# Two transformer blocks on one core: the first attention with stationary values and its softmax factors spread through DRAM, and single operations moved

## The chip, the cores and the metric

The kernel runs on one core of a Trainium2 chip. The metric is the device time of one execution in microseconds; the core's engines (TensorE for matrix products, VectorE, ScalarE, GpSimd, and SyncE, here SP, which issues nearly all DMAs) run beside each other, each in its own program order, and wait for each other by semaphores. A time is the median of several executions; one further execution is recorded by the hardware profiler, and the rows in this document come from it.

## The reference, cut to what matters

All data are float32: 1024 tokens of width 1024.

```python
# first block
h = rms_norm(x, norm_mix);  proj = h @ w_in          # aq ak av rq rk rv rg ga gr
att = sliding_window_attention(aq, ak, av, sinks)    # 8 heads of 64, 2 kv heads, window 128, alibi,
                                                     # softmax with a sink logit in the denominator
ret = head_group_norm(retention_chunkwise(rq, rk, rv)) * gain * silu(rg)
x = x + (sigmoid(ga) * (att @ w_att_o) + sigmoid(gr) * (ret @ w_ret_o)) @ w_out
h = rms_norm(x, norm_ffn)
x = rms_norm(x + (silu(h @ w_gate) * (h @ w_up)) @ w_down, final_norm)
# second block
z = rms_norm(x, g_pre_mix) @ w_in_2                  # q k v zu zv
attn = dilated_attention(q, k, v, rel_bias)          # T5 bias by relative position
sgu = spatial_gating(gelu(zu), gelu(zv), ...)
x = x + rms_norm(concat(attn, sgu) @ w_out_2, g_post_mix)
f = square(relu(rms_norm(x, g_pre_ffn) @ w_ff1)) @ w_ff2
out = x + rms_norm(f, g_post_ffn)
```

## The kernel before

**Products.** Each large product is done in three passes of a split format: an operand is cast to a high part (ScalarE, `split`, L279) and the rest is subtracted (VectorE, L281, names `wl`, `midl`), and TensorE multiplies high with high, high with low and low with high. On top of this the products use a seven-product (Strassen-like) scheme: of the 2 by 2 blocks of weights and activations, sums and differences are formed first. In `s_run` (L504 and on, matmuls at L500 to L502) the weights stand still in TensorE and the pieces are numbered 1 to 7; in `d_run` (L1169 and on, matmuls at L1199 to L1201) four accumulators run through pieces in an order given by a tuple, ORD_S, ORD_M or ORD_V. One piece of `d_run` is 48 matmuls of 512 columns.

**Weights.** `plan` lists all weight chunks (1 MB each) and pieces in the order of their use. There are two raw buffers; a chunk is loaded as soon as a buffer is free (`load_raw`, L299). A piece is split when the product before it has left room (`ahead`), at a `tick`; operations marked late are appended to a list that `flush` empties. `d_chunks` writes the combinations for one such product: `t1`, the first difference `wt = raw(0,1) - raw(0,0)`; at piece 6 `wt = raw(1,1) - wt`; at piece 3 a difference in place; and for the two orders in which piece 2 comes before piece 6 ("apart") a fourth block `wr`, loaded separately, and `t4`, `wr = wr - wt`. All of these are VectorE's, L440 in the trace. Activations of the down-projections go through DRAM: `mid_d` is stored by SP, `midr` loaded (`a_load`, L1107), and `a_split` forms their combinations (`mt`, L1138 to L1144).

**Order of work.** Nothing is scheduled by a tool: each engine's order is the order in which the code emits. Smaller work is a set of generators, and `pump` moves each of them one step, newest first, at fixed places between the large products. SP's queue is in order too: a DMA that waits for its data holds back those behind it.

**First attention.** `att1_quad` (L1275 and on) treats one block of 128 queries and four heads: 16 quads, 8 blocks by two head groups. Each goes through four steps, one per pump: scores and softmax (reductions on VectorE, L1290, exponentials on ScalarE, L1293); reciprocal of the sums (`den`, L1300) and transposes of the probabilities (L1306) into `pT`; the product with the values, `pv` (L1319), with the transposed probabilities stationary and 64 columns of values moving, and the scaling by `den` out of PSUM (L1322); two transposes of the result (L1328), a cast and a subtraction to the split format. The quads run beside the projections of retention's queries and keys (`t_unit`), with two pumps per half. The attention's output product (`ao`) comes after the retention has been begun.

**The other places that the change touches.** `bias_build` (L1420) makes the table of relative biases, stores it and copies it in DRAM to 128 rows per head (L1436) during the first FFN's `s_run`. The second FFN's `s_run` is followed by the last down-projection, four chunks e0, e8, e16 and e24. `out_chain` (L1794) is the last normalization: `osq`, `rv` and `rw` on GpSimd (L1783, L614, L615), the result on VectorE, ScalarE and GpSimd.

Of the kernel before, what the change touches and what calls it, by code (L numbers as in the profile page):

```python
# [175 lines left out]
class Kern:  # L176
# [150 lines left out]

    def get(self, key):
        while key not in self.ready:
            self.flush()  # L330
            self.split_next()
        if key in self.open:
            self.flush()
        self.n_used += 1
        return self.ready.pop(key)
# [89 lines left out]
    def d_chunks(self, w, k0, m, key, order, cols=(0, 512), n=512, late=False):  # L425
# [11 lines left out]
        if late:  # L437
            at[5] = (0, 0)
# [12 lines left out]
        def piece(p, j):  # L451
# [10 lines left out]
            def emit(r):  # L462
# [4 lines left out]
                if apart and p == (5 if late else order[1]):  # L467
# [3 lines left out]
                elif p == 3:  # L471
                    sub(blk(0, 1), blk(1, 1), blk(0, 1))
                src = (tmp[j] if p in (5, 6) or p == 4 and not apart else own[j] if p == 4 or p == 2 and apart
# [4 lines left out]
                if apart and p == 6:  # L478
# [3 lines left out]
                elif not apart and p == 1:  # L482
# [152 lines left out]
    def plan(self):  # L635
# [25 lines left out]
        self.d_chunks(a["w_ret_o"][0], 0, 4, "ro", ORD_S)  # L661
        self.d_chunks(a["w_out"][0], 0, 4, "wo", ORD_S)
# [10 lines left out]
        self.d_chunks(w2, 0, 4, "vz", ORD_V, (1024, 2048))  # L673
# [4 lines left out]
        self.d_chunks(a["w_ff1_2"][0], 0, 4, "ff", ORD_V)  # L678
# [3 lines left out]
        for k0, m in self.echunks:  # L682
            self.d_chunks(a["w_ff2_2"][0], k0, m, f"e{k0}", ORD_M)
# [296 lines left out]
    def ffn1(self, X, x1_d):  # L980
# [59 lines left out]
        for i in range(4, DFF // P, 2):  # L1040
# [5 lines left out]
            n - 7: self.bias_build,  # L1046
# [228 lines left out]
    def att1_quad(self, n, u, aq, ak, av, att):  # L1275
# [24 lines left out]
        nc.vector.reciprocal(den, den)  # L1300
        pT = self.S("pT", [P, 8, P])
# [10 lines left out]
        yield  # L1312
        pv = self.PV("pv")
        for s in range(2):
            for j in range(2):
                x = 2 * s + j
                for e in range(nh):
                    kb = n - nh + 1 + e
                    nc.tensor.matmul(pv[:, 64 * x : 64 * x + 64], pT[:, x * nh + e, :],  # L1319
                                     av[:, kb * P + 64 * s : kb * P + 64 * s + 64], start=(e == 0), stop=(e == nh - 1))  # L1320
        at = self.H("at", [P, 2, 2, 64])
        nc.vector.tensor_tensor(  # L1322
            at.rearrange("p j s d -> p s j d"), pv[:, 0:256].rearrange("p (s j d) -> p s j d", s=2, j=2),
            den.rearrange("p (s j) -> p s j", s=2)[:, :, :, None].to_broadcast([P, 2, 2, 64]), ALU.mult)
        yield
        tp = self.PM("tq").rearrange("p (a b) -> p a b", b=P)
        for j in range(2):
            nc.tensor.transpose(tp[:, j, :], at[:, j].rearrange("p s d -> p (s d)"), self.ident)  # L1328
        hi, lo = att.pair(u, n // 4)
        att.missing.discard(2 * n + u)  # L1330
        o = (n % 4) * P
        nc.scalar.copy(hi[:, :, o : o + P], tp[:, 0:2, :])
        nc.vector.tensor_tensor(lo[:, :, o : o + P], tp[:, 0:2, :], hi[:, :, o : o + P].bitcast(F32), ALU.subtract)
# [86 lines left out]
    def bias_build(self):  # L1420
        nc, a, dp = self.nc, self.a, self.dp
# [5 lines left out]
        nc.sync.dma_start(rw, a["c_row"].partition_broadcast(8))  # L1427
        R = self.S("R", [8, L_BIAS])
# [4 lines left out]
        d1 = dp.tile([8, L_BIAS], F32, name="bias_d1")  # L1433
        nc.sync.dma_start(d1, R)
        d2 = dp.tile([8, P, L_BIAS], F32, name="bias_d2")
        nc.sync.dma_start(d2, bass.AP(tensor=d1.tensor, offset=d1.offset, ap=[[L_BIAS, 8], [0, P], [1, L_BIAS]]))  # L1436
        self.bias_d = d2
# [287 lines left out]
    def ffn2(self, X, x3_d, turned):  # L1725
# [28 lines left out]
        self.d_queue(mid_d, [(k0, k0, m, ORD_M, False) for k0, m in self.echunks])  # L1754
# [243 lines left out]
```

## Time and profile before

| | us |
|---|---|
| median of three executions | 2555.37 |
| lowest and highest | 2554.02, 2561.91 |
| profiled execution, its own time | 2560.22 |
| its span | 2558.4 |

The span runs from the first to the last instruction that the profiler shows. Times in rows count from its start. "Busy" of TensorE (PE) is the time in which a matmul is under way; matmuls are pipelined, so the distance between two starts tells their cost better than one's duration. A row of the timeline gives start, duration, engine, source line, operation, result and operands, shape and count, and in brackets how long the engine had been idle before and whom it waited for. PEclk is the granted clock of TensorE as a share of 2.4 GHz.

### The profile page before, as it was taken

How to read it: one execution, taken by the hardware profiler on the slowest of the kernel's cores; microseconds unless marked ns; L12 is line 12 of the kernel's file. 1: busy time of each engine (PE TensorE's matmuls, PEld its weight loads, DVE VectorE, ACT ScalarE, POOL GpSimd, SP SyncE). 2: the span in 40 equal slices, each digit the busy share in tenths (PEclk: the TensorE clock that was granted, in tenths of full speed). 3: DMA queues.
4: the chain of work that ended last, by engine and by line, in shares of the span. 5: the costliest groups of instructions: out<-in, count | busy, mean ns of one | idle time of the engine just before them, and what ended most of it. 6: DMA issues, size and time to landing. Idle time of an engine off the chain costs nothing.

```text
span 2558.4 us, 31387 instructions
## 1 busy us (share of the span) xinstructions
PE 2488.2 (97%) x11889; PEld 2060.4 (81%) x11889; DVE 1753.5 (69%) x2741; ACT 1141.1 (45%) x1960; POOL 186.9 (7%) x252
## 2 busy tenths in 40 slices
PE   7999999999999999999999999999999999899998
PEld 5888888888778888878788877889887888788886
DVE  7654456556899845555799986666458444488888
ACT  5444445412425433333334544576436555553334
POOL 1000000000002000000000311023320000000006
PEclk9999999999999999999999999999999999999999
DMA  4233333135353122242433414233242333532334
GB/s 157 95 115 107 118 109 108 34 106 186 112 197 132 58 74 83 74 151 95 169 126 137 137 50 160 86 81 100 88 148 90 108 104 105 179 115 75 115 124 148
DMA packets 194239, 291.58 MB, mean 114 GB/s; under 512 B 27752, under 2 KB 102136, under 8 KB 194088
## 3 DMA queue, kind: packets, MB, share of 16 engines
q1 hardware_dynamic: 191784, 287.41, 33.2%
q10 hardware_dynamic: 2304, 2.16, 0.3%
q8 instruction: 94, 1.54, 0.2%
q14 instruction: 57, 0.47, 0.1%
HBM read 212.89 MB, written 80.31 MB: 115 GB/s over the span
## 4 chain that ended last, share of the span: by engine, by line
PE 75%; DVE 14%; DMA 5%; ACT 3%; issue 2%; POOL 1%; SPq 0%; DVEq 0%; ACTq 0%; POOLq 0%
PE a L500 6%; PE a L501 6%; PE a L502 6%; PE da L1201 5%; PE da L1200 5%; PE da L1199 5%; DVE wl L281 3%; PE b L501 3%; PE b L500 3%; PE b L502 3%; PE db L1200 3%; PE db L1201 3%; PE db L1199 3%; PE pv L1944 2%; DVE midl L281 2%
## 5 line engine op out<-in xcount | busy, mean ns | idle before, releaser
L500 PE MATMUL a<-midh,ws 128*128 128x512 f32 x708 | 276.6, 391 | 9.8 <-DVE f L1733 8.8
L502 PE MATMUL a<-midh,ws 128*128 128x512 f32 x708 | 276.2, 390 | 0.0
L501 PE MATMUL a<-midl,ws 128*128 128x512 f32 x708 | 276.1, 390 | 0.0
L1201 PE MATMUL da<-wh,midl 128*128 128x512 f32 x624 | 245.6, 394 | 6.3 <-DVE midl L281 6.2
L1200 PE MATMUL da<-wl,midh 128*128 128x512 f32 x624 | 245.0, 393 | 3.6 <-DVE wl L281 3.6
L1199 PE MATMUL da<-wh,midh 128*128 128x512 f32 x624 | 246.5, 395 | 0.8 <-ACT midh L279 0.8
L279 ACT CAST midh<-mt 128x1024 fp32r<-128x1024 f32 x80 | 82.9, 1036 | 246.1 <-DVE mt L1138 97.6
L1201 PE MATMUL db<-wh,midl 128*128 128x512 f32 x436 | 170.4, 391 | 2.9 <-DVE midl L281 2.8
L1199 PE MATMUL db<-wh,midh 128*128 128x512 f32 x436 | 170.4, 391 | 1.4 <-ACT midh L279 1.3
L1200 PE MATMUL db<-wl,midh 128*128 128x512 f32 x436 | 170.1, 390 | 1.6 <-DVE wl L281 1.6
L500 PEld LDWEIGHTS a<-midh,ws 128*128 128x128 f32 x708 | 133.4, 188 | 39.3 <-issue 9.6
L502 PEld LDWEIGHTS a<-midh,ws 128*128 128x128 f32 x708 | 133.3, 188 | 27.8
L501 PEld LDWEIGHTS a<-midl,ws 128*128 128x128 f32 x708 | 133.4, 188 | 27.6
L279 ACT CAST ws<-tc 128x512 fp32r<-128x512 f32 x180 | 111.4, 619 | 88.4 <-DVE tc L414 87.2
L1201 PEld LDWEIGHTS da<-wh,midl 128*128 128x128 f32 x624 | 117.9, 189 | 34.7 <-DVE midl L281 10.4
L1200 PEld LDWEIGHTS da<-wl,midh 128*128 128x128 f32 x624 | 118.1, 189 | 29.1 <-DVE wl L281 5.2
L500 PE MATMUL b<-midh,ws 128*128 128x512 f32 x360 | 140.0, 389 | 0.0
L501 PE MATMUL b<-midl,ws 128*128 128x512 f32 x360 | 140.0, 389 | 0.0
L502 PE MATMUL b<-midh,ws 128*128 128x512 f32 x360 | 140.0, 389 | 0.0
L1199 PEld LDWEIGHTS da<-wh,midh 128*128 128x128 f32 x624 | 118.1, 189 | 26.9 <-ACT midh L279 1.7
L281 DVE TENSOR_TENSOR wl<-raw,wh 128x1024 fp32r<-128x1024 f32 x117 | 136.3, 1199 | 3.7 <-ACT wh L279 3.6
L279 ACT CAST wh<-raw 128x1024 fp32r<-128x1024 f32 x121 | 120.7, 1037 | 39.5 <-DMA raw<-in_w_ff_dram 20.7
(352 smaller groups left out, 5772.5 us busy)
## 6 DMA issues: line engine op xcount, KB each, us to landing
raw<-in_w_ff_dram SPq DMA_DIRECT2D x31, 1024.0 KB, 5.1
mid_d<-f SPq DMA_DIRECT2D x108, 256.0 KB, 2.3
midr<-mid_d SPq DMA_DIRECT2D x52, 512.0 KB, 7.2
raw<-in_w_in_dram SPq DMA_DIRECT2D x22, 1024.0 KB, 5.4
x<-x_d SPq DMA_DIRECT2D x24, 512.0 KB, 5.2
raw<-in_w_up_dram SPq DMA_DIRECT2D x11, 1024.0 KB, 5.6
raw<-in_w_gate_dram SPq DMA_DIRECT2D x10, 1024.0 KB, 5.3
xt<-in_x_dram SPq DMA_DIRECT2D x16, 512.0 KB, 10.9
```

Source lines behind the costliest of these rows:

```text
L279: self.nc.scalar.copy(hi, s)
L281: e.tensor_tensor(lo, s, hi.bitcast(F32), ALU.subtract)
L500: nc.tensor.matmul(ps, hi[:, i], xh, start=(first and i == 0), stop=False, skip_group_check=True)
L501: nc.tensor.matmul(ps, hi[:, i], xl, start=False, stop=False, skip_group_check=True)
L502: nc.tensor.matmul(ps, lo[:, i], xh, start=False, stop=(i == 3), skip_group_check=True)
L1199: nc.tensor.matmul(ps, xh, wh, start=(kt == 0 and p in (1, 5, 2)), stop=False, skip_group_check=True)
L1200: nc.tensor.matmul(ps, xh, wl, start=False, stop=False, skip_group_check=True)
L1201: nc.tensor.matmul(ps, xl, wh, start=False, stop=(kt == m - 1), skip_group_check=True)
L1944: nc.tensor.matmul(pv[:, 65 * x : 65 * x + 65], pT[0:w, 2 * x + e, :], vv[0:w, 65 * x : 65 * x + 65], start=(e == 0), stop=(e == 1))
```

## The change

In the first attention the values become the stationary operand: for each of the two key blocks (`e`) and each half (`s`) one matmul loads 64 columns of values into one half of TensorE's columns, writes 64 partitions of the result, and has 256 columns of transposed probabilities moving. The result comes out feature by token, so the transposes at the end go away. The factor `den` belongs to the token, which is now the free dimension; it is stored to DRAM, transposed by the store, and loaded back spread over 64 partitions per half. ScalarE copies the product out of PSUM, and in the next step VectorE multiplies it with the factors.

Outside the attention: `t4` is put off to piece 7 for `ro`, `wo` and `ff` (`defer`); `t1` is put off to piece 5 for `vz` and `ff` (`late`) and for the first chunk of the last down-projection, e0 (`lazy`); pieces of e0 from number 5 on are not split before the `s_run` ahead of it has ended (`hold`, `release`), and the six activation loads in its last pair become two, with four in `release`; the bias table is fetched, built and spread in separate steps, the spread head by head; in the last normalization the scaling of the first half's sum is folded into a scaling of the gain.

```diff
@@ Kern
+    def hold(self, key):
+        self.cap = next(i for i, p in enumerate(self.pieces) if p[0] == key)
+
+    def release(self, n):
+        self.cap = 10 ** 9
+        self.flush()
+        self.load_raw(10 ** 9)
+        self.a_load(n)
@@ d_chunks
-    def d_chunks(self, w, k0, m, key, order, cols=(0, 512), n=512, late=False):
+    def d_chunks(self, w, k0, m, key, order, cols=(0, 512), n=512, late=False, lazy=False, defer=False):
...
-        if late:
+        if late or lazy:
             at[5] = (0, 0)
...
-                if apart and p == (5 if late else order[1]):
+                if apart and p == (5 if late else order[1]) or lazy and p == 5:
                     t1()
...
+                elif p == 7 and defer:
+                    sub(own[j], own[j], tmp.pop(j))
...
-                if apart and p == 6:
+                if apart and p == 6 and not defer:
                     def t4(t=tmp.pop(j)):
                         sub(own[j], own[j], t)
                     self.late.append(t4)
-                elif not apart and p == 1:
+                elif not apart and p == 1 and not lazy:
                     t1()
@@ plan
-        self.d_chunks(a["w_ret_o"][0], 0, 4, "ro", ORD_S)
-        self.d_chunks(a["w_out"][0], 0, 4, "wo", ORD_S)
+        self.d_chunks(a["w_ret_o"][0], 0, 4, "ro", ORD_S, defer=True)
+        self.d_chunks(a["w_out"][0], 0, 4, "wo", ORD_S, defer=True)
-        self.d_chunks(w2, 0, 4, "vz", ORD_V, (1024, 2048))
+        self.d_chunks(w2, 0, 4, "vz", ORD_V, (1024, 2048), late=True)
-        self.d_chunks(a["w_ff1_2"][0], 0, 4, "ff", ORD_V)
+        self.d_chunks(a["w_ff1_2"][0], 0, 4, "ff", ORD_V, late=True, defer=True)
-            self.d_chunks(a["w_ff2_2"][0], k0, m, f"e{k0}", ORD_M)
+            self.d_chunks(a["w_ff2_2"][0], k0, m, f"e{k0}", ORD_M, lazy=k0 == 0)
@@ ffn1
-            n - 7: self.bias_build,
+            n - 14: self.bias_fetch,
+            n - 13: self.bias_build,
+            **{n - 12 + h: (lambda h=h: self.bias_spread(h)) for h in range(8)},
@@ att1_quad
         nc.vector.reciprocal(den, den)
+        fac_d = self.dp.tile([4, P], F32, name=f"fac_d{u}_{n}")
+        nc.sync.dma_start(fac_d.rearrange("x q -> q x"), den)
...
         pv = self.PV("pv")
-        for s in range(2):
-            for j in range(2):
-                x = 2 * s + j
-                for e in range(nh):
-                    kb = n - nh + 1 + e
-                    nc.tensor.matmul(pv[:, 64 * x : 64 * x + 64], pT[:, x * nh + e, :],
-                                     av[:, kb * P + 64 * s : kb * P + 64 * s + 64], start=(e == 0), stop=(e == nh - 1))
-        at = self.H("at", [P, 2, 2, 64])
-        nc.vector.tensor_tensor(
-            at.rearrange("p j s d -> p s j d"), pv[:, 0:256].rearrange("p (s j d) -> p s j d", s=2, j=2),
-            den.rearrange("p (s j) -> p s j", s=2)[:, :, :, None].to_broadcast([P, 2, 2, 64]), ALU.mult)
+        for e in range(nh):
+            kb = n - nh + 1 + e
+            for s in range(2):
+                nc.tensor.matmul(pv[64 * s : 64 * s + 64, 0:256], av[:, kb * P + 64 * s : kb * P + 64 * s + 64],
+                                 pT[:, 2 * nh * s + e : 2 * nh * (s + 1) : nh, :], start=(e == 0), stop=(e == nh - 1))
+        both = self.H("at", [P, 2, 2, P])
+        at, fac = both[:, 0], both[:, 1]
+        nc.scalar.copy(at, pv[:, 0:256].rearrange("p (j q) -> p j q", j=2))
+        nc.sync.dma_start(fac, bass.AP(tensor=fac_d.tensor, offset=fac_d.offset, ap=[[2 * P, 2], [0, 64], [1, 2 * P]]))
         yield
-        tp = self.PM("tq").rearrange("p (a b) -> p a b", b=P)
-        for j in range(2):
-            nc.tensor.transpose(tp[:, j, :], at[:, j].rearrange("p s d -> p (s d)"), self.ident)
-        hi, lo = att.pair(u, n // 4)
+        nc.vector.tensor_tensor(at, at, fac, ALU.mult)
+        hi, lo = (x[:, :, (n % 4) * P : (n % 4) * P + P] for x in att.pair(u, n // 4))
         att.missing.discard(2 * n + u)
-        o = (n % 4) * P
-        nc.scalar.copy(hi[:, :, o : o + P], tp[:, 0:2, :])
-        nc.vector.tensor_tensor(lo[:, :, o : o + P], tp[:, 0:2, :], hi[:, :, o : o + P].bitcast(F32), ALU.subtract)
+        nc.scalar.copy(hi, at)
+        nc.vector.tensor_tensor(lo, at, hi.bitcast(F32), ALU.subtract)
@@ bias_build, split into bias_fetch (three loads), bias_build and
+    def bias_spread(self, h):
+        d1 = self.bias_row
+        self.nc.sync.dma_start(self.bias_d[h], bass.AP(tensor=d1.tensor, offset=d1.offset + h * L_BIAS, ap=[[0, P], [1, L_BIAS]]))
@@ ffn2
+        self.hold("e0:5_0")
         self.s_run(X.ops, pairs, {
...
-            len(pairs) - 1: lambda: self.a_load(6)})
+            len(pairs) - 1: lambda: self.a_load(2)})
         self.ahead, self.a_ahead = 2, 4
         X.keep.clear()
+        self.release(4)
...
                 gpo = self.bcast("gpo2", a["g_post_ffn_2"][0])
+                nc.scalar.activation(gpo, gpo, AF.Copy, scale=32.0)
...
-                    nc.gpsimd.tensor_scalar(q[:, 0:1], q[:, 0:1], 1.0 / D, EPS, op0=ALU.mult, op1=ALU.add)
@@ out_chain
-        r = yield from self.rstd(sq[:, 1:2], 1, 1.0 / D, sq[:, 0:1])
+        v, r = self.M("rv", 1), self.M("rw", 1)
+        nc.gpsimd.tensor_scalar(v, sq[:, 1:2], sq[:, 0:1], D * EPS, op0=ALU.add, op1=ALU.add)
+        nc.gpsimd.tensor_tensor(r, v, self.mhalf[:, :1], ALU.pow)
+        yield
```

## Rows read from the trace of the kernel before

**Rows 1.** The page, part 1: busy time, share of the span and instructions of TensorE

```profile
PE 2488.2 (97%) x11889; PEld 2060.4 (81%) x11889; DVE 1753.5 (69%) x2741; ACT 1141.1 (45%) x1960; POOL 186.9 (7%) x252
```

**Rows 2.** Windows, attention stage: length; busy PE, PEld, DVE, ACT, POOL; clock, DMA share, GB/s

```profile
418.00:500.00 82.00, 82.00 (x566) 72.52 (x566) 46.36 (x181) 40.84 (x147) 0.00 (x0) 1.00 0.08 27
```

**Rows 3.** Timeline of PE, the end of one quad's pump in the attention

```profile
444.18 1.90 PE L1319 MATMUL pv<-av,pT 128*128 128x64 f32 x16
445.91 0.39 PE L1328 MATMUL tq<-ident,at 128*128 128x128 f32 x2
446.06 0.48 PE L581 MATMUL mm<-zh,wh 128*128 128x512 f32 x1
```

**Rows 4.** Timeline of PE: column halves in the second block; full width in the retention

```profile
525.17 0.60 PE L1374 MATMUL po<-rvh,sd 128*128 128x256 f32 x2
525.61 0.59 PE L1376 MATMUL po<-st,qd 128*128 128x256 f32 x2
...
1547.71 1.09 PE L1845 MATMUL sgu<-wsT,yp 128*64 128x128 f32 x16
1548.73 0.50 PE L1199 MATMUL da<-wh,midh 128*128 128x512 f32 x1
```

**Rows 5.** Timeline of DVE: the reciprocals of two quads that follow each other

```profile
438.72 0.18 DVE L1300 RECIPROCAL den<-den 128x4 f32<-128x4 f32 x1
...
445.36 0.18 DVE L1300 RECIPROCAL den<-den 128x4 f32<-128x4 f32 x1
```

**Rows 6.** DMA issues: line, queue, count, KB each, median us from issue to landing

```profile
mid_d<-f SPq DMA_DIRECT2D x108, 256.0 KB, 2.3
midr<-mid_d SPq DMA_DIRECT2D x52, 512.0 KB, 7.2
```

**Rows 7.** Timeline of PE: hand-over to the last down-projection, first and second product

```profile
2234.67 0.76 PE L500 MATMUL a<-midh,ws 128*128 128x512 f32 x1 [8.82 <-DVE f L1733]
...
2238.22 0.63 PE L502 MATMUL a<-midh,ws 128*128 128x512 f32 x1
...
2239.42 0.40 PE L1199 MATMUL da<-wh,midh 128*128 128x512 f32 x1
...
2250.33 0.39 PE L1199 MATMUL db<-wh,midh 128*128 128x512 f32 x1
```

**Rows 8.** Timeline of DVE at the hand-over

```profile
2232.70 1.23 DVE L440 TENSOR_TENSOR wt<-raw,raw 128x1024 f32<-128x1024 f32 x1 [9.46 <-DMA raw<-in_w_ff_dram]
```

**Rows 9.** Timeline of SP at the hand-over

```profile
2216.70 3.83 SPq L1107 DMA_DIRECT2D midr<-mid_d  x6
...
2221.43 0.39 SPq L299 DMA_DIRECT2D raw<-in_w_ff_dram  x1
```

**Rows 10.** Windows at the hand-over, columns as in rows 2

```profile
2234.00:2238.00 4.00, 3.33 (x8) 2.68 (x9) 2.84 (x3) 3.41 (x5) 0.00 (x0) 0.50 0.17 66
```

**Rows 11.** Timeline of DVE, first projection of the second block

```profile
1468.98 2.36 DVE L440 TENSOR_TENSOR wt<-raw,raw 128x1024 f32<-128x1024 f32 x2
```

**Rows 12.** Timeline of PE, first projection of the second block

```profile
1471.73 0.44 PE L140 MATMUL tp<-ident,xn 128*128 128x128 f32 x2 [1.82 <-DVE zr L146]
```

**Rows 13.** Timeline of DVE, before the second FFN

```profile
1923.48 1.29 DVE L1716 SCALAR_TENSOR_TENSOR x<-y,rw,x 128x1024 f32<-128x1024 f32 x1 [0.44 <-POOL rw L615]
```

**Rows 14.** Timeline of DVE, retention's output projection

```profile
682.75 1.22 DVE L440 TENSOR_TENSOR wr<-wr,wt 128x1024 f32<-128x1024 f32 x1
```

**Rows 15.** Timeline of PE, retention's output projection

```profile
685.16 0.50 PE L1200 MATMUL da<-midl,wh 128*128 128x512 f32 x1 [3.12 <-DVE midl L281]
```

**Rows 16.** Waits of DVE, 685 to 800: us in total, times, longest us

```profile
DVE midl L281 <- ACT midh L279: 4.7, 6, 1.2
```

**Rows 17.** Timeline of PE in the first FFN

```profile
1140.97 0.50 PE L500 MATMUL c<-zh,ws 128*128 128x512 f32 x1 [1.09 <-ACT ws L279]
```

**Rows 18.** Timeline of DVE at the end

```profile
2547.01 0.76 DVE L1803 SCALAR_TENSOR_TENSOR yg<-yg,rw,x 128x512 f32<-128x512 f32 x1 [2.33 <-POOL rw L615]
```

**Rows 19.** Timeline of POOL at the end

```profile
2542.25 0.51 POOL L1783 TENSOR_SCALAR osq<-osq 128x1 f32<-128x1 f32 x1
```

More of the change, by code (lines that the diff above doesn't have):

```diff
@@ L1417, in retention, with bias_fetch @@
         return [vload()] + [chunk(c) for c in range(8)] + [finish()]
-    def bias_build(self):
-        nc, a, dp = self.nc, self.a, self.dp
+    def bias_fetch(self):
+        nc, a = self.nc, self.a
         rb = self.cp.tile([32, 8], F32, name="rb")
@@ L1427, in bias_build @@
         nc.sync.dma_start(rw, a["c_row"].partition_broadcast(8))
+        self.bias_in = rb, oh, rw
+    def bias_build(self):
+        nc, a, dp = self.nc, self.a, self.dp
+        rb, oh, rw = self.bias_in
         R = self.S("R", [8, L_BIAS])
@@ L1432, in bias_build @@
             nc.vector.scalar_tensor_tensor(R[:, lo:hi], ps[0:8, : hi - lo], 8.0, rw[:, lo:hi], op0=ALU.mult, op1=ALU.add)
[L1433 to L1437, printed above, removed]
+        self.bias_row = dp.tile([8, L_BIAS], F32, name="bias_d1")
+        nc.sync.dma_start(self.bias_row, R)
+        self.bias_d = dp.tile([8, P, L_BIAS], F32, name="bias_d2")
+    def bias_spread(self, h):
+        d1 = self.bias_row
+        self.nc.sync.dma_start(self.bias_d[h], bass.AP(tensor=d1.tensor, offset=d1.offset + h * L_BIAS, ap=[[0, P], [1, L_BIAS]]))
     def bias_load(self, off, n, name, heads=range(8)):
```

## The prediction

> **What bounds the kernel now.** I read the page first: TensorE is busy for 97% of the span [rows 1]; the other 70 us are start, tail and stalls. Then the windows of the attention stage: TensorE is busy for every one of its 82 us at full clock, VectorE and ScalarE for about half, DMA for a twelfth [rows 2]. So there only TensorE's own work counts, and a microsecond taken from it comes off the span. Last I took TensorE's idle times one by one from its timeline; each edit outside the attention lies beside one of them, and what is to be seen there is which instruction stands in VectorE's order ahead of the one that TensorE waits for.
>
> **The attention.** One quad's `pv` group takes from 444.18 to 445.91, 1.73 us, and the two transposes of the result 0.15 more [rows 3]: 1.88 us. The change drops the transposes and replaces eight matmuls of 64 columns by four of 256 on alternating column halves. No row shows this shape. The nearest one also loads 64 weight columns into alternating halves: sixteen records of 128 columns in 1.02 us [rows 4], and the new group streams the same number, eight of 256. Without overlap, four full-width matmuls of 256 columns (0.44 us each, two records) would take 1.76 [rows 4]; with perfect halves 0.88. In-order issue lets the second record of one half run beside the first of the other: four matmuls make five steps of 0.22, 1.1 us; eight of 0.11 make nine, 0.99, near the 1.02 seen. I take 1.1. Fourteen quads have eight matmuls, the first of each of the two head groups four. Full quads save 0.78 each, 10.9; the short ones (0.87 + 0.15, against three steps, 0.66) 0.7 together: **11.5 us**, bounds 2 (14 times 0.12 and a little) and 15 (14 times 1.0, twice 0.58).
>
> Other engines: ScalarE gets one copy of 256 columns per quad, VectorE multiplies from SBUF instead of PSUM; both have half their time free [rows 2], so nothing. SP gets a store of the factors and a load of their spread, 32 DMAs. The store waits for the reciprocal, the load for the store; behind them on SP stand the reloaded queries, needed only for the second half of the quads, and the weight loads, while DMA stands nearly still [rows 2]. VectorE's multiply stands two pumps behind the reciprocal. A pump is now 6.64 us, reciprocal to reciprocal [rows 5]; 0.8 shorter, two are 11.7 us. A store to DRAM lands in 2.3 us and a load of 512 KB in 7.2 [rows 6], 9.5 together, and the new ones carry less; the cover holds, at a price of nothing. Were it gone, VectorE would stop inside the pump, with the score reductions of the next quad behind it. In the last quads the loads of the retention values (8 DMAs) go into the queue ahead of the factors; I count that as up to 3 us of the upper end.
>
> The rows show stores of long runs only; this one writes 512 elements of 4 bytes. The Trainium skill, "DMA: Bandwidth & Descriptors", section "Rules for kernel authors", speaks against it: a non-contiguous last dimension becomes one descriptor per element, and an outermost dimension of two confines a transfer (here the load) to two engines. By the rows the two transfers cost nothing; by that page they are slower by an amount that no row has. "TensorEngine Tiling (Array Packing)" of the Trainium skill, section "Theoretical Speedup", gives up to twofold for 64 columns, which is the 0.88 end, and 15 us in the sum; the overlap in the row stays short of that.
>
> **The hand-over to the last down-projection.** TensorE stands for 8.82 us [rows 7] for an evacuation that is behind `wt` in VectorE's order; `wt` waits 9.46 us for a weight chunk [rows 8]. That chunk was issued behind six activation loads [rows 9]. Afterwards TensorE runs at half clock [rows 10], 1.2 GHz: the first nine starts take 3.55 us, 0.44 apart; at full clock 48 matmuls take 10.91, 0.227 apart [rows 7], so ten lose 2.1. Gross 10.9. The edits delay `wt` behind the evacuations, hold the pieces that need it, and let two activation loads instead of six go ahead. What is late next: the four other loads now stand on SP behind the last two stores of the stage, behind an addition and four activations of 512 columns, each about half of the 1.2 us that 1024 take [rows 8]: they go out some 3 us after TensorE begins the first product and land 7.2 later or earlier [rows 6]; `mt` for the second product waits for them in VectorE's order, with the weight parts behind it. Two sums, two residues and two weight residues of 1.2 us each (the durations of rows 8 and 14) then meet a second product that begins 10.9 us after the first [rows 7]. I estimate 4.2 us of new stall: **6.7 net** (10.9 less 4.2), between 3 and 10.9.
>
> **The reordered weight combinations.** In the second block's first projection two `wt` subtractions of 2.36 us stand ahead of the copy that the transposes wait for, 1.82 us [rows 11, 12]. Moved to piece 5 they fall into idle time of VectorE while it waits for the next transposes: **2.2** (a second stall of the kind follows), between 0 and 4. In the second FFN the same subtraction is followed by a wait for GpSimd's `rw` [rows 13], so the copy comes no earlier: **0.2**, at most 1.8, as in rows 12. In the two projections with `defer`, two `wr` subtractions stand ahead of the late `midl`, a stall of 3.12 us [rows 14, 15]; a smaller one recurs in the next. But from 685 to 800 VectorE waits only for ScalarE's casts, 4.7 us in six waits, never for TensorE [rows 16]: it is the bound there, the subtraction still has to be done, and what TensorE gains early it waits later. **0.7**, between 0 and 4.
>
> **Bias and tail.** The 3.6 MB spread now goes out in one DMA, and a weight load comes behind it: a stall of 1.09 us [rows 17]. In eight parts over eight pairs it goes: **1.0**. At the end VectorE waits 2.33 us for GpSimd [rows 18], with some `osq` operations of about 0.51 ahead of it [rows 19]; without two or three of them 1.2 less. Against that, ScalarE now scales the gain at the last chunk's start and waits for its load, up to 7.2 us [rows 6], most of which passes before ScalarE comes to it. The casts behind it come later and VectorE, full there, waits: 1.5. Together **0.3 slower**, between -1.4 and +3.
>
> **Sum.** 11.5 + 6.7 + 2.2 + 0.2 + 0.7 + 1.0 - 0.3 = 22.0 us. The profiled execution took 2560.2 us, 1.8 above its span and 4.8 above the median of 2555.4; against it the change gives 2538.2, and in terms of the median **2533**.
>
> **Rivals.** (1) The halves don't overlap: the attention gives 2 instead of 11.5, 2543. For it: the matmuls are four-byte and accumulate in pairs; against it: so many records in 1.02 us in rows 4. (2) Only the attention counts: the stalls are moved, not removed, as in the stage where VectorE is the bound [rows 16], and the second product takes back all of the hand-over: 2544. (3) Every stall goes: 10.9 for the hand-over, 4 for the first projection, 3 for the deferred ones, the tail 1.4: 2523. (4) Slower: store and load of the factors together take more than 11.7 us. Then VectorE stops in each pump and the pump takes on the excess: at 15 us, 3.3 for each of 16 quads is 53 us, less 22 won: 2586. It begins to lose at 13.1 us, where 16 times 1.4 eats the gain. For it: the short runs; against it: the 9.5 us of far larger transfers. That is the rule of the Trainium skill named above, as a mechanism.
>
> **How the numbers follow.** About 0.3% (7.7 us) is what a measurement of this kernel can tell from no change: faster means below 2547.7. Forecast 0.60, rivals 0.12, 0.12, 0.10 and 0.06. The forecast and (3) are faster, (1) and (2) in some four of five cases, else the same: 0.88 faster, 0.06 same, 0.06 slower. All terms at their good ends give 2517, all at their bad ends 2553; leaving out one case in ten on either side, 2520 to 2548 takes in the first three rivals.
>
> **What would show it.** The `pv` group at about 1.1 us and no transposes behind it; a pump of 5.9 us; no VectorE wait for `fac`; the 8.8 us stall gone and two short ones at the second product of the last down-projection; the 1.82 and 1.09 gone; the 3.12 shortened, with new short ones later in the same stage. A `pv` group of 1.7 us, VectorE waiting for `fac`, or ScalarE waiting long for `gpo` would make the prediction wrong.

## The result and the profile after

The changed kernel takes **2589.5 us** (median of four runs, 2585.6 to 2593.0) against 2555.1 for the kernel before: ratio 1.011, 95% interval 1.008 to 1.015. It is slower; I had predicted 2533 and 2520 to 2548.

The first reading is by stages. In each trace I took the start of the first output projection behind the attention (`ao`) and of the first scores of the second block's attention (`sc`), and the end of the span:

| kernel | ao starts | from ao to sc | from sc to the end | span |
|---|---|---|---|---|
| before | 570.2 | 1114.5 | 873.7 | 2558.4 |
| after | 600.9 | 1116.1 | 873.2 | 2590.2 |

Of the 31.8 us, 30.7 were lost before `ao`. The windows of the attention stage in the changed kernel, the answer to [rows 2] (columns as there):

```profile
418.00:500.00 82.00, 66.78 (x363) 47.76 (x361) 33.27 (x138) 33.83 (x123) 0.00 (x0) 0.88 0.20 43
```

TensorE, which was busy for all of the 82 us, now works for 66.8 of them, at a granted clock of 0.88. DMA has a share of 0.20 and moves 43 GB/s: it is neither full nor idle. The timeline of PE has what was hoped for, and the first stall, in one pump (compare [rows 3]):

```profile
430.29 1.08 PE L1336 MATMUL pv<-pT,av 128*64 128x256 f32 x8
431.30 0.50 PE L594 MATMUL mm<-midh,wh 128*128 128x512 f32 x1
...
441.54 1.01 PE L1280 MATMUL sc<-kst,qst 128*128 128x256 f32 x3 [7.12 <-DVE nm L1305]
```

The `pv` group takes 1.01 us from start to start, instead of 1.73, and no transposes follow. But the next scores come 7.12 us late, for a reduction on VectorE. The timeline of VectorE has the reason at the multiplication with the factors (L1343):

```profile
443.27 0.41 DVE L1343 TENSOR_TENSOR at<-at 128x256 f32<-128x256 f32 x1
453.89 0.43 DVE L1343 TENSOR_TENSOR at<-at 128x256 f32<-128x256 f32 x1 [6.35 <-DMA at<-fac_d]
457.83 0.42 DVE L1343 TENSOR_TENSOR at<-at 128x256 f32<-128x256 f32 x1
470.07 0.42 DVE L1343 TENSOR_TENSOR at<-at 128x256 f32<-128x256 f32 x1 [7.94 <-DMA at<-fac_d]
```

and SP's timeline has what the load of the factors (L1341) stands behind:

```profile
436.84 0.51 SPq L1341 DMA_DIRECT2D at<-fac_d  x1
442.84 0.35 SPq L1318 DMA_DIRECT2D fac_d<-den  x1
443.29 0.51 SPq L1341 DMA_DIRECT2D at<-fac_d  x1
447.03 0.35 SPq L1318 DMA_DIRECT2D fac_d<-den  x1
452.79 0.51 SPq L1341 DMA_DIRECT2D at<-fac_d  x1
457.38 0.35 SPq L1318 DMA_DIRECT2D fac_d<-den  x1
457.83 0.51 SPq L1341 DMA_DIRECT2D at<-fac_d  x1
```

Read the two together. The load issued at 443.29, right behind the next quad's store, is waited for until 453.89, 10.6 us; the one at 457.83, again right behind a store, until 470.07, 12.2 us. Those at 436.84 and 452.79, which SP could issue only when their own store had landed, are used at 443.27 and 457.83 without a wait, 6.4 and 5.0 us on. So up to 500 us every second pump stalls. The DMA view from 442 to 458 us (GB/s, slices of 0.4 us):

```profile
GB/s 0 0 0 0 4 1 15 49 49 15 0 0 0 5 1 7 3 0 0 0 0 0 13 49 49 49 31 0 0 0 18 28 51 38 51 46 51 31 13 0
```

A load of this shape moves at up to 51 GB/s here. By size, the load issued at 443.29 moves in two pieces, some 51 KB up to 446.0 us and 76 KB from 450.8, with 4.8 us between them in which nearly nothing moves; the one issued at 452.79 moves in one piece, from 454.0 to 457.6.

The waits from 400 to 605 us (us in total, times, longest), of VectorE and PE, and the DMA issue of the store (KB each, median us to landing):

```profile
DVE at L1343 <- DMA at<-fac_d: 64.8, 11, 9.9
...
PE sc L1280 <- DVE nm L1305: 14.4, 4, 7.1
PE mm L596 <- DVE wl L281: 5.9, 2, 5.4
PE tp L1374 <- DVE sd L1380: 4.1, 1, 4.1
PE tp L1324 <- DVE pT L1329: 3.9, 4, 2.8
...
fac_d<-den SPq DMA_DIRECT2D x16, 2.0 KB, 9.0
```

2 KB take 9.0 us to land, where 256 KB took 2.3 [rows 6]. VectorE waits 64.8 us for the factors; what the next scores, the retention and the weights lose by that on TensorE is 29 us (14.4 + 5.9 + 4.1 + 3.9 and a smaller one of 0.7); in the kernel before, PE's waits in that stage are 0.6 in all. Four reciprocals on from 442.60 comes the one at 473.31, 7.68 us a quad, where it was 6.64 [rows 5].

### The profile page after: what moved, and what is told of

Its sections match the earlier page's. It is cut to its first block, busy times and chain, and to the rows that moved or that the text cites. A ratio compares the mean times of both kernels' runs of the same rounds, so it can differ in the third digit from the quotient of the medians.

```text
span 2590.2 us, 31167 instructions
## 1 busy us (share of the span) xinstructions
PE 2495.8 (96%) x11737; PEld 2044.0 (79%) x11737; DVE 1752.2 (68%) x2741; ACT 1147.3 (44%) x1977; POOL 180.9 (7%) x244
## 2 busy tenths in 40 slices
DMA packets 204886, 293.69 MB, mean 113 GB/s; under 512 B 36352, under 2 KB 112784, under 8 KB 204736
## 4 chain that ended last, share of the span: by engine, by line
PE 69%; DVE 15%; DMA 9%; ACT 3%; issue 2%; SPq 1%; POOL 1%; DVEq 0%; ACTq 0%; POOLq 0%
PE a L513 6%; PE a L514 6%; PE a L515 6%; PE da L1216 5%; PE da L1214 5%; PE da L1215 5%; DVE wl L281 4%; DMA at<-fac_d 3%; PE b L514 3%; PE b L515 3%; PE b L513 3%; PE db L1216 3%; PE db L1215 3%; PE db L1214 3%; DVE midl L281 2%
## 5 line engine op out<-in xcount | busy, mean ns | idle before, releaser
L1216 PEld LDWEIGHTS da<-wh,midl 128*128 128x128 f32 x624 | 117.5, 188 | 34.5 <-DVE midl L281 10.5
```

The source lines that it names most:

```text
L1216: nc.tensor.matmul(ps, xl, wh, start=False, stop=(kt == m - 1), skip_group_check=True)
```

## Experiments

Theory **A**: the store of 512 runs of 4 bytes takes 9 us and holds up the load behind it. Rivals: **B**, the load is slow by itself, since its outermost dimension is 2; **C**, any round trip through DRAM is too long for two pumps; **D**, the loss comes from the other edits. All edits are against the changed kernel where nothing else is said; ratios are to runs of the kernel before on the same chip.

### The attention alone, and everything but it

`att_only` is the kernel before with the new `att1_quad`; `rest_only` the changed kernel with the old one.

> The kernel before with the new attention alone; no other edit. Theory A (the store of the factors, 512 runs of 4 bytes, lands about 9 us after issue, and a load that is issued behind it on the same queue waits for it, so that VectorE and then TensorE stand at the multiplication): all of the loss is here; the first ao product starts near 602 us as in the changed kernel (571.5 before), and the time is about 2555 + 31 = 2586 us (2580 to 2592). Rival D (the loss comes from the other edits, and the attention is near what was predicted): about 2544 us. The prediction's own terms gave 2543.

> The changed kernel with the attention of before; all other edits kept. Theory A: ao starts near 572 us as before, and the rest of the landmarks says that the other edits come out near nothing (hand-over to the second half's last layer about 7 us gained, its last chunk about 6 lost, the stage of vz about 2 lost): 2551 to 2559 us. The prediction's terms for these edits sum to -10.5: 2545 us. Rival D: 2575 us or more.

`att_only`: 2597.3 us, 1.014 (1.010 to 1.018), `ao` at 604.0, 5 us above the range for A. `rest_only`: 2554.6, 0.997 (0.995 to 1.000), `ao` at 570.9. D falls: all of the loss is in the attention. Without the new attention, the windows of the stage are those of before again:

```profile
418.00:500.00 82.00, 82.00 (x570) 72.64 (x569) 47.04 (x183) 41.41 (x149) 0.00 (x0) 1.00 0.08 25
```

The other edits together put the span 6.8 us ahead, 2551.6 against 2558.4 (1 to 14 by the ratio): more than the near nothing that the landmarks of the changed kernel had suggested, less than the 10.5 of my terms. By the table's landmarks that is 1.2 from `ao` to `sc` (1113.3), 6.3 behind it (867.3), and a loss of 0.7 before `ao`. But 3.0 of the 6.3 lie between `sc` and the first product of the second FFN, where no edit stands: TensorE's clock there was 0.96 in the execution before and 0.98 in this one. So the edits by themselves are worth some 4 us.

### Dense rows for the store

```diff
-        nc.sync.dma_start(fac_d.rearrange("x q -> q x"), den)
+        tf = self.PM("tq")
+        nc.tensor.transpose(tf[0:4, 0:P], den, self.ident)
+        dt = self.H("dt")[:, 0:P]
+        nc.vector.tensor_copy(dt[0:4, :], tf[0:4, 0:P])
+        nc.sync.dma_start(fac_d, dt[0:4, :])
```

> The changed kernel, but the factors are transposed on TensorE to four rows of 128 (one transposition and one small copy on VectorE more for each quad) and stored as 4 runs of 512 bytes; the load is as it was. Theory A (the store's 4-byte runs are the cost): the store lands in 2 to 3 us, no wait of VectorE for the factors, ao starts at 562 to 568 us, the time is 2546 to 2555 us. Rival B (the load is slow by itself, its outermost dimension being 2): VectorE still waits for the load, ao near 600 us, 2584 to 2592 us. Rival C (two pumps are too short for any round trip by way of DRAM): some stalls left, 2560 to 2580 us.

2599.9 us, 1.014 (1.010 to 1.018): no gain, and yet not the rival's picture. No wait for the factors is left among VectorE's; the waits of PE from 400 to 605 us show a new one that I had put in:

```profile
PE tq L1319 <- DVE den L1315: 34.7, 15, 3.1
PE tq L1319 <- ACT z L1308: 2.4, 1, 2.4
```

The transposition needs the reciprocal, which VectorE has just begun to work on, and TensorE, in order, waits 2.3 us for it on average, 37 us in the 16 quads. As a test of A that run was badly placed. `dense2` puts the same lines one pump later, behind the `pv` products, and the load one pump behind that:

```diff
+        tf = self.PM("tq")
+        nc.tensor.transpose(tf[0:4, 0:P], den, self.ident)
...
+        nc.sync.dma_start(fac_d, dt[0:4, :])
+        yield
         nc.sync.dma_start(fac, bass.AP(...))
         yield
```

> As the run that stored four dense rows, but the transposition of the factors stands one pump later, behind the products with the values, where the reciprocals are long ready, and the load one pump later still, the multiplication a pump after that. In the first such run no DMA was waited for, but TensorE waited 2.4 us in each quad for the reciprocal. Theory A (the 512 runs of 4 bytes hold up the queue): store and load land inside a pump of about 6 us each, no stall, quads follow each other in 6.1 to 6.4 us (6.64 before, 7.2 to 7.5 in the changed kernel), ao at 562 to 572 us, the time is 2548 to 2558 us. Rival B (the load is slow by itself) or C (any round trip is too long): VectorE waits for the factors, 2570 us or more.

2542.8 us, 0.993 (0.990 to 0.997), `ao` at 559.6. The stage's windows, two reciprocals, and VectorE's waits for the factors, in that order:

```profile
418.00:500.00 82.00, 82.00 (x510) 61.37 (x511) 52.43 (x209) 46.90 (x165) 0.00 (x0) 1.00 0.20 65
...
430.80 0.18 DVE L1315 RECIPROCAL den<-den 128x4 f32<-128x4 f32 x1
436.71 0.18 DVE L1315 RECIPROCAL den<-den 128x4 f32<-128x4 f32 x1
...
DVE at L1348 <- DMA at<-fac_d: 4.8, 4, 1.5
```

TensorE is full again, at full clock, a quad takes 5.91 us, and 64.8 us of waiting have become 4.8. Time, `ao` and pace all came out better than the ranges that I had set for A.

### One pump more, another queue, another shape of the load

Is it the store's form, or only the extra pump? `cover1` has the extra pump and keeps the store of 4-byte runs:

```diff
         nc.sync.dma_start(fac, bass.AP(...))
         yield
+        yield
```

> The changed kernel with one pump more between the load of the factors and the multiplication, the store of 4-byte runs kept. If it is throughput (theory A: a store keeps the queue for about 7 us and every quad brings one, against a pump of about 6 us): the pace of the quads stays near 7 us, the delays pile up, and the time is 2575 to 2592 us. Rival C (only the latency of one round trip of about 19 us, which two pumps do not cover): the wait is gone, 2550 to 2560 us.

2567.1 us, 1.001 (0.998 to 1.005), `ao` at 585.5. VectorE still waits:

```profile
DVE at L1344 <- DMA at<-fac_d: 50.6, 12, 11.2
```

At `ao` half of the loss goes (15.3 us behind the kernel before instead of 30.7), which neither side had said: the delays do not pile up for good, and they are not gone. With equal cover from reciprocal to multiplication, the dense rows are 24 us faster than the 4-byte runs. So C alone is not the cause.

`actq` issues the store from ScalarE's queue (`nc.scalar.dma_start`):

> The changed kernel with the store of the factors issued from ScalarE's queue; everything else is as it was, two pumps of cover. If the load only suffers from standing behind the next store on its own queue: the load lands about 2.5 us after its issue, what is left of the round trip is 9 + 2.5 us against two pumps of 12, and the time is 2550 to 2562 us. If the elements of 4 bytes load the DMA engines themselves, whatever the queue: the load still waits, 2575 us or more.

2602.6 us, 1.015 (1.010 to 1.020), slower still:

```profile
DVE at L1343 <- DMA at<-fac_d: 78.0, 12, 16.7
```

The stores land in 9.9 us there too, and the load, with no store ahead of it on its own queue, is late as before: one that SP issues at 449.16, 1.7 us behind ScalarE's store of 447.47, is used at 459.18, 10.0 us on and after a wait. So it is not the place in SP's queue; the two share something behind the queues. This agrees with the Trainium skill, "DMA: Bandwidth & Descriptors", section "Issuing engines are not separate DMA queues", by which DMAs of all queues interleave on the same 16 engines. No run here shows the engines one by one. The DMA share stayed low (0.20 in the stage of the changed kernel), and between the two pieces of the delayed load above nearly nothing moved; so what exactly is occupied for 9 us remains open.

`wide` cuts the load in two, partitions outermost:

```diff
-        nc.sync.dma_start(fac, bass.AP(..., ap=[[2 * P, 2], [0, 64], [1, 2 * P]]))
+        for s in range(2):
+            nc.sync.dma_start(fac[64 * s : 64 * s + 64], bass.AP(..., ap=[[0, 64], [1, 2 * P]]))
```

> The changed kernel with the load cut in two, each with its 64 partitions outermost, instead of one load whose outermost dimension is 2. Theory A (the load waits behind the store): nothing changes, 2583 to 2597 us. Rival B (the shape of the load is what is slow): the waits of VectorE for the factors go, 2550 to 2565 us.

2588.0 us, 1.009 (1.007 to 1.012): as A has it. But the profiled execution, the fastest of the ten (2575.8), had `ao` at 594.1, and

```profile
DVE at L1344 <- DMA at<-fac_d: 59.0, 13, 8.2
```

so the shape of the load may be worth a little. B falls as the main cause only.

### Fewer runs, without TensorE

`row16` stores the factors as they lie, 128 runs of 16 bytes, and loads whole rows:

```diff
-        nc.sync.dma_start(fac_d.rearrange("x q -> q x"), den)
+        nc.sync.dma_start(fac_d, den)
...
-        nc.sync.dma_start(fac, bass.AP(..., ap=[[2 * P, 2], [0, 64], [1, 2 * P]]))
+        nc.sync.dma_start(fac[:, 0:510], bass.AP(..., ap=[[2, 2], [0, 64], [1, 510]]))
...
-        nc.vector.tensor_tensor(at, at, fac, ALU.mult)
+        nc.vector.tensor_tensor(at, at, fac.rearrange("p (q x) -> p x q", x=4)[:, 0:2, :], ALU.mult)
```

> The changed kernel with the factors stored as they lie, 128 runs of 16 bytes, and loaded as whole rows of 2 KB (twice the bytes), the multiplication picking every fourth number; no work more on TensorE or VectorE, and the pumps as in the changed kernel. If the cost of the store goes by its number of runs (theory A: 512 runs took 9 us, some 2 of them a fixed part, so 128 runs some 2 + 7/4 = 4 us): store and load fit into two pumps, waits of VectorE for the factors under 10 us in all, ao at 560 to 572 us, the time 2543 to 2558 us. If it goes by anything else (the bytes, the DRAM round trip itself): 2570 us or more.

2559.0 us, 0.998 (0.996 to 1.001), `ao` at 574.7. DMA issues from 435 to 470 us, and VectorE's wait from 400 to 605:

```profile
fac<-fac_d SPq DMA_DIRECT2D x6, 255.0 KB
fac_d<-den SPq DMA_DIRECT2D x6, 2.0 KB, 2.0
...
DVE at L1342 <- DMA fac<-fac_d: 37.1, 15, 6.5
```

The same 2 KB in a quarter of the runs land in 2.0 us instead of 9.0. That settles A against its rivals: the bytes and the round trip are as before, the runs are not. I had expected 4 us, a fixed part and a share for each run; 2.0 is less, so a price per run is not shown. Nor is it shown which property of the runs costs: their number, their length, and their place in DRAM (the 16-byte runs lie one behind the other, the 4-byte ones were transposed) change together here. The bounds for the waiting (10 us), `ao` (572) and the time (2558) were missed, since the load, twice as large, had become the long part. While it runs, the DMA view of these 35 us has mostly 49 to 53 GB/s. Now B's price shows, in `best`: the same rows, the load cut in two as in `wide` (with two edits elsewhere, below).

> What the runs point to, together: the changed kernel with the factors stored as 128 rows of 16 bytes, the load cut in two with the partitions outermost (in the earlier run of 16-byte rows the load of 255 KB with an outermost dimension of 2 moved at 51 GB/s and VectorE waited 37 us for it in 15 quads), the scaling of the last gain issued late, and the late difference of vz undone. Theory A with the load's shape as the rest: no wait for the factors is left but in the first quads, a quad every 5.8 to 6.0 us, ao at 556 to 563 us; the stage from 1470 to 1560 us gives back about 2 us; the time is 2533 to 2542 us. If the load's shape is not what held the 16-byte rows up: VectorE still waits 1 to 2 us a quad, ao at 570 us or later, 2548 us or more.

Its DMA issues from 435 to 470 us, and VectorE's wait, as above:

```profile
fac<-fac_d SPq DMA_DIRECT2D x12, 127.5 KB, 3.0
fac_d<-den SPq DMA_DIRECT2D x7, 2.0 KB, 1.4
...
DVE at L1343 <- DMA fac<-fac_d: 1.2, 1, 1.2
```

37.1 us of waits have become 1.2, a quad takes 5.90 us, `ao` starts at 558.2, the earliest of all. This is a round trip through DRAM under two pumps, so C falls outright. With an outermost dimension of two the load moved at 51 GB/s, with the partitions outermost at up to 173. The rule of the Trainium skill that I had named beside the store, that an outermost dimension of two confines a transfer to two engines ("DMA: Bandwidth & Descriptors", "Rules for kernel authors"), agrees; how many engines took part, no view shows. In the changed kernel that term was hidden under the store's, as `wide` showed. As a whole, `best` took 2544.9 us, 0.994 (0.992 to 0.997), above its range; the last section says what of that can be seen.

### The factors by TensorE

`spread` has no DMA for the factors: ScalarE copies the reciprocals out to 128 columns, and two products with the identity turn them.

```diff
+        nc.scalar.copy(dw.rearrange("p j (s d) -> p s j d", s=2), den...to_broadcast([P, 2, 2, 64]))
...
+        for j in range(2):
+            nc.tensor.matmul(fac[:, P * j : P * j + P], dw[:, j, :], self.ident, start=True, stop=True)
```

> The changed kernel without the round trip: the reciprocals are spread to 128 columns by a copy on ScalarE, and two products with the identity on TensorE turn them feature-major beside the multiplication. Theory A: no wait for a DMA is left at the multiplication; a quad costs TensorE 1.1 us for the values and about 0.5 us for the factors against 1.73 + 0.15 before, so ao starts at 566 to 572 us and the time is 2550 to 2558 us. If the stationary values on column halves or the feature-major multiplication cost by themselves: ao at 585 us or later, 2570 us or more.

2550.4 us, 0.995 (0.992 to 0.998), `ao` at 566.2. The group and the two products:

```profile
435.43 1.08 PE L1335 MATMUL pv<-pT,av 128*64 128x256 f32 x8
436.45 0.71 PE L1342 MATMUL tq<-ident,dw 128*128 128x128 f32 x4
436.91 0.48 PE L594 MATMUL mm<-midh,wh 128*128 128x512 f32 x1
```

1.02 and 0.46 us, 1.48 instead of 1.88 a quad: 0.40 times 16 is 6.4, against 4.8 measured at `ao`. The other 1.6 us no view here explains; PE's waits from 400 to 605 us are 1.4 us in all.

### The last chunk and the hand-over

Both are edits of `dense2`. `tail_late` moves the scaling of the last gain (`gpo`) behind the chunk's first four products; `no_hand` takes out `hold`, `release`, `lazy` and the two activation loads instead of six.

> The version with dense rows one pump later (2543 us, span 2540.8), with one more edit: the scaling of the last gain by 32 on ScalarE, which in the changed kernel stands ahead of the last chunk and waits 7.2 us for its load, is issued behind the chunk's first four products. If that wait is what costs the last chunk its small stalls: they go, 3 to 5 us less, span 2536 to 2538 us. If the last chunk's loss is the slower splits at its end (3.6 us of wait for wl): no change, 2540 to 2542.

> The version with dense rows one pump later (span 2540.8), without the hand-over edits: no hold and release, the first chunk's sum not put off, six operands fetched at once as before. My term for this edit was a gain of 6.7 us: the stall of some 9 us at the second product of the first chunk comes back and 2 to 4 us of small ones go, span 2546 to 2549 us. If the edit only moves the wait: 2540 to 2542.

`tail_late`: 2539.0 us, 0.993 (0.990 to 0.996), span 4.3 shorter than that of `dense2`. ScalarE's timeline, in the changed kernel and then in `tail_late`:

```profile
2501.93 1.06 ACT L1791 ACTIVATE gpo<-gpo 128x1024 f32<-128x1024 f32 x1 [7.24 <-DMA gpo<-in_g_post_ffn_dram]
```

```profile
2455.25 1.05 ACT L1807 ACTIVATE gpo<-gpo 128x1024 f32<-128x1024 f32 x1
```

The wait is gone. The time from the start of the last chunk's first group of second-set products (`db`) to that of its last group of first-set ones (`da`) was 43.5 us before, 45.9 in the changed kernel and 45.7 in `dense2`; it is 43.5 again. From there to the end it was 36.0, 37.9 and 38.1; it is 36.7. So 3.6 of the 4.3 us lie in the last chunk (2.2 and 1.4), more than the sum of PE's short waits that went there (1.2 us up to 2505). The wait of 3.6 us for a late weight residue (3.5 now) stayed; the rival had that part, but not the loss.

`no_hand`: 2549.6 us, 0.997 (0.993 to 1.000), 6.9 slower than `dense2` by the medians and 9.3 by the profiled spans (2550.1, just above its range). But 5.3 of the 9.3 lie between `sc` and the second FFN, where no edit stands and the clock was 0.95 instead of 0.98. The edit's own stretch, from the `d` group at the end of the `s_run` to the start of the fourth group of e0, took 48.1 us against 43.6: 4.6. The stall of [rows 7] is back:

```profile
2221.84 0.77 PE L513 MATMUL a<-midh,ws 128*128 128x512 f32 x1 [7.85 <-DVE f L1760]
```

## Why the prediction was wrong

**The attention: one step failed.** TensorE's side came as worked out: `pv` in 1.01 us (I took 1.1), a pump of 5.9 us as soon as nothing was in the way, and 11.3 us won at `ao` in `dense2` against `rest_only` (559.6 against 570.9), 12.8 in `best`, which puts no work of its own on TensorE; I had 11.5 (its parts add up to 11.6). Rival (1), no overlap of the halves, falls. The step that failed is the cover: "A store to DRAM lands in 2.3 us and a load of 512 KB in 7.2 [rows 6], 9.5 together, and the new ones carry less; the cover holds, at a price of nothing." The rows measured stores of long runs, and I let bytes stand for time. The store took 9.0 us for its 512 runs, and 2.0 in 128. The packets under 512 bytes rose from 27752 to 36352, 8600 more, of which 16 times 512 are 8192. That agrees with the rule of the Trainium skill that I had named beside it, one descriptor per element ("DMA: Bandwidth & Descriptors", "Rules for kernel authors"). I had no row for the price and so took none, where the bound should have been open upwards.

A second assumption stood inside that step: that store and load of one quad are a chain by themselves. In fact one quad's load is issued 0.45 us behind the next quad's store, and reciprocal to multiplication took 25 us (428.74 to 453.89) for the two pumps.

**The size.** 30.0 us lost against `rest_only` at `ao`, where 11.3 were to be won: 41 us. TensorE's waits are 29 of these; the other 12 stand beside a clock of 0.88 from 418 to 500 us and 0.93 from 500 to 575, at most 15 us (0.12 of 82 and 0.07 of 75). Rival (4) had the mechanism and, with 2586, nearly the time; it had a chance of 0.06. Its detail was off: the excess was not 3 us in every pump but up to 9.9 us of VectorE in every second. The 15 us of its round trip were an example, and 25 were measured, so that 2586 came so near is luck.

**The hand-over: right, within what the traces tell.** I had 10.9 gross less 4.2 of new stall, 6.7. From that `d` group to the first group of e0 it took 16.5 us before and 5.4 in all eleven versions with the edit: 11.0 won. From the second group to the third it took 10.9 before, 14.4 in the changed kernel and up to 17.4 in the others: 3.5 to 6.5 lost. Over the edit's own stretch that is 7.5 us in the changed kernel and 5.9 on average (48.6 in the three traces without, 42.7 in the eleven with). That the medians of `dense2` and `no_hand` differ by 6.9 is partly luck, since most of their spans' difference lies elsewhere. The 8.8 us stall went, and short ones came at the second product, as said, on PE in the changed kernel:

```profile
2276.15 0.50 PE L1216 MATMUL db<-wh,midl 128*128 128x512 f32 x1 [1.15 <-DVE midl L281]
2278.36 0.50 PE L1214 MATMUL db<-wh,midh 128*128 128x512 f32 x1 [1.01 <-ACT midh L279]
2279.62 0.50 PE L1216 MATMUL db<-wh,midl 128*128 128x512 f32 x1 [0.53 <-DVE midl L281]
```

**The reordered weight combinations and the bias: each came out differently.** Between `ao` and `sc` I had 2.2 + 0.7 + 1.0 = 3.9. That stretch took 1114.5 us before and 1113.3, 1114.5, 1114.0, 1115.1 and 1117.9 in the five versions with these edits that are not disturbed in the attention, and all of PE's waits in it sum to 25.2 us before and 25.2 after: in sum nothing. Cut at the same marks in all fourteen traces, the stages tell the edits apart:

| edit, and the stretch | without it | with it | I had |
|---|---|---|---|
| `defer` for `ro`, `wo`: first `db` of retention's projection to the first transposes of `xn` | 145.0 | 144.9 to 145.0 | 0.7 won |
| bias in parts: first `c` to first `d` of the first FFN's `s_run` | 340.8, 343.0 | 339.1 to 339.4 | 1.0 won |
| `vz`, first part: first transposes of `xn` to first `db` | 37.1 to 38.2 | 36.2 to 38.0 | 2.2 won |
| `vz`, second part: from there to the first `sgu` | 43.1 | 44.4 to 44.5 | - |
| `ff`: first `da` to the first `c` of the second `s_run` | 81.8, 81.7 | 79.5 | 0.2 won |

The stall of 1.09 us [rows 17] is gone, and at least 1.4 us with it. `defer` gave nothing, as Rival (2) has it: the waits moved. `vz` shows no gain and a loss of 1.3: its stall of 1.82 us [rows 12] shrank to 0.48, the second one beside it grew from 2.13 to 2.33, and behind them 1.3 were lost, which `best`, with this edit undone, has back (I had expected 2):

```profile
1501.49 0.66 PE L140 MATMUL tp<-ident,xn 128*128 128x128 f32 x4 [0.48 <-DVE zr L146]
1507.96 0.94 PE L140 MATMUL tp<-ident,xn 128*128 128x128 f32 x4 [2.33 <-DVE zr L146]
```

`ff` won 2.3 us where I had 0.2. I had written that a wait for GpSimd's `rw` follows the subtraction [rows 13], "so the copy comes no earlier". The subtraction had made that wait. In the kernel before, VectorE, GpSimd and the stall on PE:

```profile
1920.69 2.35 DVE L440 TENSOR_TENSOR wt<-raw,raw 128x1024 f32<-128x1024 f32 x2
1920.89 1.07 POOL L614 TENSOR_SCALAR rv<-ssq 128x1 f32<-128x1 f32 x1
1922.04 1.41 POOL L615 TENSOR_TENSOR rw<-rv,mhalf 128x1 f32<-128x1 f32 x1
1929.76 0.66 PE L140 MATMUL tp<-ident,y 128*128 128x128 f32 x4 [1.84 <-DVE zr L146]
```

and GpSimd in the changed kernel, with no subtraction beside it:

```profile
1958.26 0.19 POOL L627 TENSOR_SCALAR rv<-ssq 128x1 f32<-128x1 f32 x1
1958.54 0.55 POOL L628 TENSOR_TENSOR rw<-rv,mhalf 128x1 f32<-128x1 f32 x1
```

The same two operations on one column took 2.5 us beside the subtraction and 0.7 without it. `x` on VectorE began 2.9 us behind the sum `ssq` before and 1.1 after, and the stall of 1.84 us on PE is gone.

**The tail: mis-sized.** I had 0.3 slower, as 1.5 lost by the scaling and 1.2 won on GpSimd. By the same two marks the last chunk lost 2.4 and 1.9 us, 4.3, and `tail_late` gets 3.6 of it back. I had written of ScalarE's wait for its load that "most of which passes before ScalarE comes to it"; all 7.24 us stood in front of ScalarE, with the casts behind it. VectorE's wait for GpSimd at the end did shrink, from 2.33 us [rows 18] to 0.46.

**Together.** `dense2` is this change with the store mended: 17.6 us of span ahead of the kernel before, 16.9 by its ratio (interval 9 to 25). By stretches, from start to start:

| stretch | before | `dense2` | won |
|---|---|---|---|
| start to `ao` | 570.2 | 559.6 | 10.6 |
| `ao` to `sc` | 1114.5 | 1114.5 | 0.0 |
| `sc` to the second FFN: no edit | 233.4 | 230.0 | 3.4 |
| `ff` | 81.8 | 79.5 | 2.3 |
| hand-over | 49.2 | 43.6 | 5.6 |
| last chunk and end | 79.6 | 83.8 | -4.2 |

The two stretches that are left out agree to 0.1 us. So 14.2 of the 17.6 us stand where edits stand; the 3.4 go with the clock, 0.96 against 0.98.

## What to carry to other kernels

A DMA's time is read from a row of the same shape, runs and outermost dimension, and not from one of more bytes: 2 KB took 9.0 us in 512 runs of 4 bytes, 2.0 in 128 of 16, and a load of 255 KB moved at 51 GB/s with an outermost dimension of 2, at up to 173 with the partitions outermost. When a round trip is put under pumps, lay out the queue for two rounds at once: whose load stands behind whose store. If a wait is on an engine that all pumps share, such as VectorE here, a late transfer stops everything behind it, and a test that moves the wait to TensorE, as `dense` did, proves nothing until the operation is placed where its input is old.

The fastest version of the runs, by its median, is `tail_late`: the stationary values, dense rows for the factors one pump later, and the gain scaled late, 0.993 of the kernel before and 0.98 of the changed one (2539.0 against 2589.5).

## What the runs showed of the chip that I had not expected

The store of 4-byte runs delays a load that another engine's queue issues: in `actq` the load of 449.16 was used 10.0 us on, after a wait, where in the changed kernel the loads without a store just ahead took 5.0 and 6.4 at most. And a subtraction of 2.35 us on VectorE made two one-column operations on GpSimd take over three times as long, 2.5 us instead of 0.7.

The second block's attention, which no experiment touched, ran at either level of TensorE's clock in the same code. The profiled execution of `best` shows this in its windows (columns as in [rows 2]), `tail_late` the other case:

```profile
1740.00:1750.00 10.00, 9.85 (x68) 8.36 (x68) 6.47 (x29) 6.62 (x19) 2.52 (x7) 0.92 0.30 78
1750.00:1760.00 10.00, 10.00 (x49) 9.15 (x48) 4.87 (x21) 3.85 (x10) 2.37 (x7) 0.50 0.34 78
...
1790.00:1800.00 10.00, 10.00 (x42) 8.60 (x42) 3.51 (x14) 4.45 (x12) 6.67 (x6) 0.50 0.28 89
```

```profile
1740.00:1800.00 60.00, 58.21 (x464) 51.30 (x462) 41.23 (x168) 40.32 (x103) 32.10 (x49) 1.00 0.38 118
```

In `best` TensorE was busy for all but 0.15 us of the ten in which the clock began to fall, and then stood at 0.50, 1.2 GHz, for some 50 us with every window full; in `tail_late` it idled 1.8 us in the same stretch and kept 2.4 GHz. From `sc` to the end that is 883.4 us against 862.2. The changed kernel has a shorter fall of the kind (0.50 from 1820 to 1830 us): from `sc` to the second FFN it took 238.5 us against the 230.4 of `rest_only`, enough to hide the 6.3 us that `rest_only` gains behind `sc` (873.2). So a difference between single executions behind `sc` says little by itself, and whether `best` is slower than `tail_late` for another reason than this is left open.
